# First expert slot narrowed to 64 places, the most loaded expert to 96, on raw weights

## The chip, the cores and the metric

The program runs on one core of a Trainium2 chip. The metric is the device time of one execution in microseconds (us), here the median of three runs. TensorE is called PE, VectorE DVE, ScalarE ACT, SyncE SP; SP issues all the DMA loads that matter here.

## The reference, cut to what matters

Two layers run over 256 latent tokens of width 1024. The change touches only the last part, the channel mixer of layer 1, a mixture of eight experts, each with three weight matrices of 1024 x 3584 float32:

```python
def moe_swiglu(x, w_router, w_gate, w_up, w_down):
    xt = x.reshape(-1, D)
    logits = (xt @ w_router).astype(jnp.float32)
    top_v, top_i = lax.top_k(logits, TOP_K)            # TOP_K = 2 of 8 experts
    top_w = jax.nn.softmax(top_v, axis=-1)
    gates = jnp.sum(jax.nn.one_hot(top_i, N_EXPERTS) * top_w[..., None], axis=1)
    y = jnp.zeros_like(xt)
    for e in range(N_EXPERTS):
        y = y + gates[:, e:e + 1] * swiglu(xt, w_gate[e], w_up[e], w_down[e])
    return y

def swiglu(x, w_gate, w_up, w_down):
    return (jax.nn.silu(x @ w_gate) * (x @ w_up)) @ w_down
```

All weights of all eight experts are read: 8 x 3 x 14.7 MB = 352 MB.

## The kernel before, in words

**Slots.** The experts are worked off in eight slots, one after the other. Slot 0 always holds expert 0, so that its weights can be loaded before the routing is known; slots 1 to 7 take the other experts by their token counts, the loads of these slots read the expert's number from a register on SP (`slot_expert`, a TENSOR_LOAD of `ordi`). The letters of `MODES` (L78) give each slot's width. L (wide) has 128 places; its weights are split by ACT and DVE (`split`, L168 and L169) into a high and a low float32r half, and PE multiplies three times (`mm3`, L232 to L234). S has 64 places, M has 96 (three groups of 32); both use the float32 weights as they were loaded ("raw"), with the tokens as the stationary side in 64 or 32 columns of the array and the weights streaming through it (`columns`, L1504). S and M are ranked: the smallest counts get S, the next M, the rest L. If a count is over the slot's places, a branch behind the slots (`tc.If(over > 0)`) runs all eight experts once more as wide ones for the rest of the tokens.

**Units.** A slot's weights come in 42 units of 1 MiB, 336 in all. Slot by slot and chunk by chunk (`CH`, columns of 1024, 1024, 1024, 512): gate, then up of a chunk (8 units, in the last chunk 4), then the down rows of the chunk before it (4 units, or 2). The last chunk's down units therefore stand behind the first gate and up of the next slot. PE goes through the units in that order; between them stand the transposes of the activations, the scatter of the previous slot's result, and the gather of the next slot's tokens, which are handed out one step per unit (`extras`).

**Buffers.** `moe_load` gives each unit a place in SBUF in the order that the generator `stages` yields. Places that lie there from the first eight units on are `wsx`, `hc`, `xgb0`, `xgb1`, `yh` and three called `wst2`, `wst4`, `wst5` (`ORDER`); the first unit lies in `sg` and `at`. Behind them `FILLS` names the places that come free when the attention layer ends. After that the loads go round the places: `RAW`, `yh` and `FIRSTS`, and, once the last wide slot's units are all loaded, also the three `wd` tiles, which until then hold the split halves. `yh` and `side1` leave the round after 40 units (`YHU`), because they are needed for results. A load can be issued only when the unit that lay in its place has been read to the end: by the split in a wide slot, by PE in a raw one. SP works off its loads in order.

**Order.** In this part of the program the order on each engine is the order in which the code is written (`manual_schedule` with `ROUTE` and `MOE`).

Of the kernel before, what the change touches and what calls it, by code (L numbers as in the profile page):

```python
# [8 lines left out]
def _quiet(msg, *args, **kwargs):  # L9
# [6 lines left out]
F32 = mybir.dt.float32  # L16
F32R = mybir.dt.float32r
I32 = mybir.dt.int32
AF = mybir.ActivationFunctionType
OP = mybir.AluOpType  # L20
# [3 lines left out]
P = 128  # L24
# [12 lines left out]
UNIT = 2048  # L37
# [15 lines left out]
LOOK = 2  # L53
NHALF = 5
HB = 5
FIRSTS = ('wst',) * 3 + ('xgb0', 'side0', 'wx', 'wst3', 'hx', 'side1', 'xgb1')
FILLS = 'wst wst hx0 wst xgb0 side0 wx wst3 hx1 side1'
LH = 5
RAW = ('wsx', 'wst5', 'hc', 'wst2', 'wst4')
ORDER = ('xgb0', 'xgb1', 'wsx', 'wst5', 'hc', 'wst2', 'wst4', 'yh')  # L60
PLACE = ('xgb', 'wst2', 'wst4', 'wst5', 'sg', 'at', 'yh')
TACT = 0, 2
# [8 lines left out]
BEGIN = "v a a n00 w0 s1 c t3 t2 m00 s1 a q3 a q2 W1 f n10 a n01 n11 b m10 a a n21 m01 s1 s1 a n20 n30 n31 a m11 a s1 m21 n41 a n40 m31 a w1 n51 m20 m30 s1 s1 n50 a m40 a n60 s1 s1 a n61 m41 m51 a m50 m60 m61 n70 n71 m71 m70"  # L71
START = {mybir.EngineType.PE, mybir.EngineType.SP}
WARM = 4, 4
YHU = 40
GY = 2
TMM = (3,)

MODES = "LSLMSMMS"  # L78
PARTS = {"S": (64, 1), "M": (32, 3)}
SLOTCAP = [P if m == "L" else PARTS[m][0] * PARTS[m][1] for m in MODES]  # L80
SLOTRANK = [-1] + [sum(MODES[1:].count(x) for x in "SML"[:"SML".index(m)]) + MODES[1:s + 1].count(m) - 1
                   for s, m in enumerate(MODES) if s]

# [48 lines left out]
def body(tc, nc, I, out, dbg=None):  # L132
    ctxs = []

    def pool(**kw):
        return tc.tile_pool(**kw)

    V, A, PE = nc.vector, nc.scalar, nc.tensor
# [3 lines left out]
    with top:  # L142
        con = top.enter_context(pool(name="con", bufs=1))
        psp = top.enter_context(pool(name="psum", bufs=1, space=PSUM))
        wst = top.enter_context(pool(name="wst", bufs=3))
        hpool = tc.tile_pool(name="hpool", bufs=1, side="right")
        hp = hpool.__enter__()
        cur = {}
# [88 lines left out]
        ph = top.enter_context(pool(name="all", bufs=1))  # L237
# [56 lines left out]
        hx = [ph.tile([P, 4, 256], F32, name=f"hx{i}", bufs=1) for i in range(2)]  # L294
        hc = ph.tile([P, DT, 256], F32, name="hc", bufs=1)
# [94 lines left out]
        G = [[con.tile([P, DT, 2], F32, name=f"G{l}{n}") for n in range(2)] for l in range(2)]  # L390
# [128 lines left out]
        def mod(l, i, d, s):  # L519
            return modT[l][:, 8 * i + d, s:s + 1]  # L520
# [131 lines left out]
        first = ada_first()  # L652
# [201 lines left out]
        for g in range(7):  # L854
# [15 lines left out]
            for which in ("g", "u"):  # L870
                if g == 0 and which == "g":
                    u = []
                    ps = []
# [17 lines left out]
                for fh in range(2):  # L891
                    u = stream.take(2)
                    feed(FEED.get((g, which, fh), 1))
                    for f2 in range(2):
                        ps = mm_ps()
# [221 lines left out]
        units = list(first_units)  # L1117
        early = {n: mp.tile([P, SIZES.get(n, UNIT)], F32, name=n, bufs=1) for n in PLACE}
# [13 lines left out]

        def stages():
            i = len(loaded)
            split_ends = max(j for j, u in enumerate(units) if u[0].mode == "L")
            for n in FIRSTS[FIRSTS.index("side1") + 1:]:
                i += 1
                yield n
            while True:
                for n in RAW + ("yh",) + FIRSTS + (("wd",) * (NHALF - 2) if i > split_ends else ()):  # L1140
                    if n == "wd" and "rest" in cur:
                        continue
                    if n != "wx" and (n not in ("yh", "side1") or i < YHU):
                        i += 1
                        yield n

# [62 lines left out]
        moe_stream = Halves(first_units)  # L1209
# [47 lines left out]
        side = ph.tile([P, 4096], F32, name="side", bufs=1)  # L1257
        early["side0"], early["side1"] = side[:, :UNIT], side[:, UNIT:]
        sums = early["side1"].rearrange("p (c d) -> p c d", c=2)
        early["wx"] = ph.tile([P, UNIT], F32, name="w", bufs=4)  # L1260
        early["hx"] = [ph.tile([P, UNIT // 2], F32, name=f"hx{i}", bufs=1) for i in range(2)]
        fills = FILLS.split()
        split_unit = source(units[len(loaded) + [n for n in fills if n != "hx0"].index("hx1")])
        parts = []
        for n in fills:
            if n[:2] == "hx":
                src, (k, n_) = split_unit
                i = int(n[2])
# [16 lines left out]
        for c in range(2):  # L1285
            V.scalar_tensor_tensor(lg[:, c, :], lgp[:, NE * c:NE * c + NE], rt[:, c:c + 1], wrb[:, 1, :],
                                   op0=OP.mult, op1=OP.add)
# [81 lines left out]

        def gather(ex, first=False):  # L1370
            if ex.mode != "L":
                yield from gather_raw(ex)
                return
            oh = s2t()[:, :2 * P].rearrange("p (c s) -> p c s", c=2)
            one_hot(oh, ex, 2)
            for _ in range(GY):
                yield
            xg = wtile().rearrange("p (i d s) -> p i d s", i=2, d=DT)
            ex.xg = xg
            n = 2 if first else 4  # L1380
            held = []
            for d0 in range(0, DT, n):
                tmp = s2t()[:, :n * P]
                ps = mm_ps() if first and d0 % 4 else tp_ps()
                for a in range(n):
                    for c in range(2):
                        h, d = divmod(d0 + a, 4)
                        PE.matmul(ps[:, a * P:(a + 1) * P], acct[c, h][:, d * P:(d + 1) * P], oh[:, c, :],
                                  start=(c == 0), stop=(c == 1))
                yield  # L1390
                for a in range(n):
                    dst, src, g, b = tmp[:, a * P:(a + 1) * P], ps[:, a * P:(a + 1) * P], G[1][1][:, d0 + a, 0:1], mod(1, 3, d0 + a, 0)
                    if first and a:
                        V.tensor_scalar(dst, src, g, b, op0=OP.mult, op1=OP.add)
                    else:
                        A.activation(dst, src, AF.Identity, bias=b, scale=g)
                tmp = tmp.rearrange("p (d s) -> p d s", s=P)
                A.copy(xg[:, 0, d0:d0 + n, :], tmp)
                held.append((d0, tmp))
                if not first or d0:  # L1400
                    low(xg, *held.pop(0))
                yield
            if first:
                low(xg, *held.pop(0))
                moe_stream.ahead(NHALF)
# [2 lines left out]
            n = tmp.shape[1]  # L1408
            V.tensor_sub(xg[:, 1, d0:d0 + n, :], tmp, xg[:, 0, d0:d0 + n, :])

        def gather_raw(ex):
            n = SLOTCAP[ex.col]
            oh = s2t()[:, :2 * n].rearrange("p (c s) -> p c s", c=2)
            one_hot(oh, ex, 2, n)
            for _ in range(GY):
                yield
            ex.tile = ph.tile([P, UNIT], F32, name="w", bufs=4)
            ex.xg = ex.tile[:, :DT * n].rearrange("p (d s) -> p d s", d=DT)
            for d0 in range(0, DT, 4):
                ps = tp_ps()  # L1420
                for d in range(d0, d0 + 4):
                    for c in range(2):
                        h, i = divmod(d, 4)
                        PE.matmul(ps[:, (d - d0) * n:(d - d0 + 1) * n], acct[c, h][:, i * P:(i + 1) * P], oh[:, c, :],  # L1424
                                  start=(c == 0), stop=(c == 1))
                yield
                scaled_rows(ex, ps, d0, 4, n)

        def back_raw(ex):
            dg = s2t().rearrange("p (a c t) -> p a c t", a=2, c=2)  # L1430
# [13 lines left out]
                V.scalar_tensor_tensor(ex.oht[:, i, :], held[:, :256], C("place" + ex.mode)[:, i:i + 1], held[:, 256:],  # L1444
                                       op0=OP.is_equal, op1=OP.mult)

        def scaled_rows(ex, ps, d0, k, n):
            for d in range(k):
                A.activation(ex.xg[:, d0 + d, :], ps[:, d * n:(d + 1) * n], AF.Identity,
                             bias=mod(1, 3, d0 + d, 0), scale=G[1][1][:, d0 + d, 0:1])  # L1450

        def gather_back(ex):
            if ex.mode != "L":
# [261 lines left out]
        with tc.manual_schedule(engines=MOE):  # L1715
# [4 lines left out]
            ex = order[-1]  # L1720
            y = scaled(ex)
            ps = {(c, h): tp_ps() if h else mm_ps() for c in range(2) for h in range(2)}
# [8 lines left out]
        with tc.If(over > 0):  # L1731
# [3 lines left out]
            rest = [Expert("L", e, [past, sel, selr, gates], e) for e in range(NE)]  # L1735
# [38 lines left out]
```

## Time and profile before

| | us |
|---|---|
| median of 3 runs | 1734.12 (1733.98 to 1734.18) |
| the profiled execution | 1732.13 |
| its span, first to last instruction | 1730.0 |
| granted PE clock over the span | 0.993 |
| PE busy | 1686.2 |
| DVE busy | 887.3 |
| ACT busy | 564.0 |
| read from HBM | 474.65 MB |

The busy time of PE is no measure of how full it is: a matmul that waits in the pipeline for its weights counts as busy. What tells the stages of the expert part apart is the rate of the DMA queues, and the times at which each slot gets through its first gate and up.

### The profile page before, as it was taken

The numbers are of one execution on the slowest core, as the hardware profiler recorded it, in microseconds if no ns is written. First come the engines' busy times: TensorE is split into PE (matmuls) and PEld (weight loads), VectorE is DVE, ScalarE is ACT, GpSimd is POOL, SyncE is SP. The second block draws the span as 40 slices with busy tenths as digits, with TensorE's granted clock in tenths as the row PEclk, the third lists the DMA queues.
The fourth block names the chain that finished last, engine by engine and source line by source line (L and its number), as shares of the span: only waits on it lengthen the run. The fifth ranks groups of instructions, "written<-read, shape, count | busy, mean of one in ns | idle before, by whom it ended". The sixth has DMA issues, their size and how long they took to land.

```text
span 1730.0 us, 32514 instructions
## 1 busy us (share of the span) xinstructions
PE 1686.2 (97%) x13735; PEld 1195.5 (69%) x13735; DVE 887.3 (51%) x1638; ACT 564.0 (33%) x1006; POOL 37.2 (2%) x33
## 2 busy tenths in 40 slices
PE   7999999999999999999899999999999999999997
PEld 4678988788787879979787447876654456656532
DVE  5579677767687767786887318862001010020021
ACT  4434532222222234685676126751000001001000
POOL 0000000000000000050000000000000000000000
PEclk9999999999999999999999999999999999999998
DMA  9765345544455432327888999999999999999994
GB/s 309 266 223 191 98 147 195 169 148 153 139 170 189 152 122 98 99 78 284 299 313 298 404 403 409 403 409 408 402 376 405 406 408 402 407 377 345 373 403 170
DMA packets 193736, 477.88 MB, mean 276 GB/s; under 512 B 9096, under 2 KB 68656, under 8 KB 192560
## 3 DMA queue, kind: packets, MB, share of 16 engines
q1 hardware_dynamic: 193584, 475.73, 74.8%
q8 instruction: 110, 1.80, 0.4%
q14 instruction: 42, 0.34, 0.1%
HBM read 474.65 MB, written 1.05 MB: 275 GB/s over the span
## 4 chain that ended last, share of the span: by engine, by line
PE 89%; DVE 4%; DMA 4%; issue 1%; ACT 1%; SPq 1%; POOL 0%; DVEq 0%; ACTq 0%
PE mm L1504 31%; PE mm L232 16%; PE mm L233 16%; PE mm L234 16%; PE tp L1424 1%; PE tp L1606 1%; DMA wst<-in_moe_w_gate_dram 1%; DMA xgb<-in_moe_w_gate_dram 1%; PE mm L1021 1%; PE mm L458 1%; PE tp L1555 1%; DVE wd L169 1%; DVE w L169 1%; DMA wst<-in_ada_w_dram 1%; DMA side<-in_ctx_dram 1%
## 5 line engine op out<-in xcount | busy, mean ns | idle before, releaser
L1688 DVE TENSOR_TENSOR sg<-sg,mm 128x512 f32<-128x512 f32 (+2 forms) x50 | 27.5, 580 | 408.3 <-PE mm L1504 408.3
L232 PE MATMUL mm<-b,w 128*128 128x512 f32 (+1 forms) x560 | 206.2, 368 | 0.0
L233 PE MATMUL mm<-b,w 128*128 128x512 f32 (+1 forms) x560 | 205.0, 366 | 0.0
L234 PE MATMUL mm<-b,w 128*128 128x512 f32 (+1 forms) x560 | 204.7, 366 | 0.0
L169 DVE TENSOR_TENSOR w<-wst,w 128x512 fp32r<-128x512 f32 (+1 forms) x201 | 145.2, 764 | 76.4 <-ACT w L168 76.0
L168 ACT CAST w<-wst 128x512 fp32r<-128x512 f32 (+1 forms) x201 | 127.5, 683 | 173.9 <-PE mm L233 129.8
L1504 PE MATMUL mm<-wst,w 128*32 128x256 f32 (+3 forms) x2544 | 177.1, 373 | 6.6 <-issue 6.6
L494 DVE SCALAR_TENSOR_TENSOR s<-wst,cT,s 128x512 f32<-128x512 f32 x224 | 153.3, 748 | 9.1 <-DMA wst<-in_ada_w_dram 9.1
L1504 PEld LDWEIGHTS mm<-wst,w 128*32 128x32 f32 (+1 forms) x2544 | 90.5, 115 | 79.2 <-issue 49.5
L1557 ACT COPY s<-tp 128x512 f32<-128x512 f32 (+2 forms) x33 | 16.4, 498 | 325.3 <-PE tp L1555 266.3
L232 PEld LDWEIGHTS mm<-b,w 128*128 128x128 f32 x560 | 105.7, 189 | 23.0 <-ACT side L168 4.2
L234 PEld LDWEIGHTS mm<-b,w 128*128 128x128 f32 x560 | 105.6, 189 | 17.0
L233 PEld LDWEIGHTS mm<-b,w 128*128 128x128 f32 x560 | 105.7, 189 | 16.7 <-DVE b L169 0.2
L1504 PE MATMUL mm<-wst,s 128*32 128x256 f32 (+1 forms) x1240 | 93.9, 403 | 1.3 <-issue 0.7
L232 PE MATMUL mm<-b,side 128*128 128x512 f32 (+1 forms) x240 | 90.9, 379 | 0.0
L234 PE MATMUL mm<-b,side 128*128 128x512 f32 (+1 forms) x240 | 90.2, 376 | 0.0
L233 PE MATMUL mm<-b,side 128*128 128x512 f32 (+1 forms) x240 | 90.0, 375 | 0.0
L232 PE MATMUL mm<-w,b 128*128 128x512 f32 (+1 forms) x224 | 79.3, 355 | 0.0
L233 PE MATMUL mm<-w,b 128*128 128x512 f32 (+1 forms) x224 | 78.1, 350 | 0.2 <-DVE w L169 0.2
L234 PE MATMUL mm<-w,b 128*128 128x512 f32 (+1 forms) x224 | 77.9, 348 | 0.0
L1504 PEld LDWEIGHTS mm<-wst,s 128*32 128x32 f32 (+1 forms) x1240 | 45.5, 113 | 45.6 <-issue 22.5
L1685 ACT ACTIVATE sg<-mm 128x512 f32<-128x512 f32 (+2 forms) x50 | 23.6, 510 | 149.8 <-PE mm L1504 149.8
(402 smaller groups left out, 3059.0 us busy)
## 6 DMA issues: line engine op xcount, KB each, us to landing
wst<-in_moe_w_gate_dram SPq DMA_DIRECT2D x55, 1024.0 KB, 13.2
wst<-in_moe_w_up_dram SPq DMA_DIRECT2D x51, 1024.0 KB, 14.1
wst<-in_moe_w_down_dram SPq DMA_DIRECT2D x51, 1024.0 KB, 14.8
wst<-in_ada_w_dram SPq DMA_DIRECT2D x40, 1024.0 KB, 5.2
xgb<-in_moe_w_gate_dram SPq DMA_DIRECT2D x18, 1024.0 KB, 11.7
wst<-in_ffn_w_gate_dram SPq DMA_DIRECT2D x14, 1024.0 KB, 5.0
wst<-in_ffn_w_up_dram SPq DMA_DIRECT2D x14, 1024.0 KB, 5.0
wst<-in_ffn_w_down_dram SPq DMA_DIRECT2D x14, 1024.0 KB, 5.1
```

The lines of the kernel that those rows point to most:

```text
L168: A.copy(hi, src)
L169: V.tensor_sub(lo, src, hi)
L232: PE.matmul(ps, sh, mh, start=start, stop=False)
L233: PE.matmul(ps, sh, ml, start=False, stop=False)
L234: cur["pe"] = PE.matmul(ps, sl, mh, start=False, stop=stop).ins
L458: PE.matmul(ps[j:j + 32, :], ones[:, :32], acc_[s], start=True, stop=True)
L494: V.scalar_tensor_tensor(acc_[s], u[:, k, :], c_, acc_[s], op0=OP.mult, op1=OP.add)
L1021: PE.matmul(ps[64 * par:64 * par + 64, :256], vt[:, kc, 64 * kvh:64 * kvh + 64], pT[:, kc, par].rearrange("p a b -> p (a b)"), start=(kc = ...
L1424: PE.matmul(ps[:, (d - d0) * n:(d - d0 + 1) * n], acct[c, h][:, i * P:(i + 1) * P], oh[:, c, :], start=(c == 0), stop=(c == 1))
L1504: PE.matmul(ps[n * g:n * g + n, c0:c0 + w], x, wrow[:, w * g:w * g + w], start=start and first, stop=stop and last)
L1685: A.activation(x, p, AF.Silu)
L1688: V.tensor_mul(x, x, p)
```

## The change

`MODES` goes from `LSLMSMMS` to `SMSMMSMS`: slot 0 gets 64 places instead of 128, slot 1 96 instead of 64, slot 2 64 instead of 128. No wide slot is left in the normal course, so no expert weight is split. The `wd` tiles hold raw units from the start, and a second `w` tile (`wy`) takes one unit of the first filling. The round of places becomes one table (`CYCLE`), and `LEAVE` says after how many units a place leaves it: `yh` after 70, `side1` after 40. The first gather goes through `gather_raw`; its eight evictions with scale and bias alternate between DVE and ACT.

```diff
-FIRSTS = ('wst',) * 3 + ('xgb0', 'side0', 'wx', 'wst3', 'hx', 'side1', 'xgb1')
-FILLS = 'wst wst hx0 wst xgb0 side0 wx wst3 hx1 side1'
+CYCLE = ('xgb0', 'xgb1', 'wsx', 'wst5', 'hc', 'wst2', 'wst4', 'yh', 'wst', 'wst', 'wst', 'wd', 'wd', 'wd', 'side0', 'wst3',
+         'hx', 'side1')
+FILLS = 'wst wst hx0 wst wd wd wd side0 wx wy wst3 hx1 side1'
-RAW = ('wsx', 'wst5', 'hc', 'wst2', 'wst4')
-YHU = 40
+LEAVE = {'yh': 70, 'side1': 40}
-MODES = "LSLMSMMS"
+MODES = "SMSMMSMS"
...
-                for n in RAW + ("yh",) + FIRSTS + (("wd",) * (NHALF - 2) if i > split_ends else ()):
-                    if n == "wd" and "rest" in cur:
+                for n in CYCLE:
+                    if n == "wd" and (i <= split_ends or "rest" in cur):
                         continue
-                    if n != "wx" and (n not in ("yh", "side1") or i < YHU):
+                    if i < LEAVE.get(n, i + 1):
                         i += 1
                         yield n
...
-        early["wx"] = ph.tile([P, UNIT], F32, name="w", bufs=4)
+        for n in ("wx", "wy"):
+            early[n] = ph.tile([P, UNIT], F32, name="w", bufs=4)
...
-        def scaled_rows(ex, ps, d0, k, n):
+        def scaled_rows(ex, ps, d0, k, n, first):
             for d in range(k):
-                A.activation(ex.xg[:, d0 + d, :], ps[:, d * n:(d + 1) * n], AF.Identity,
-                             bias=mod(1, 3, d0 + d, 0), scale=G[1][1][:, d0 + d, 0:1])
+                dst, src, g, b = ex.xg[:, d0 + d, :], ps[:, d * n:(d + 1) * n], G[1][1][:, d0 + d, 0:1], mod(1, 3, d0 + d, 0)
+                if first and d % 2 == 0:
+                    V.tensor_scalar(dst, src, g, b, op0=OP.mult, op1=OP.add)
+                else:
+                    A.activation(dst, src, AF.Identity, bias=b, scale=g)
```

SP's queue at the end of the attention layer, where the places of the first filling come free (`hx` is half a unit, the numbers only tell tiles apart). Before:

```order
L179 DMA hx_7210<-in_moe_w_down_dram 128x1024
L179 DMA wst<-in_moe_w_gate_dram 128x2x1024
L179 DMA xgb<-in_moe_w_up_dram 128x2x1024
L179 DMA side<-in_moe_w_up_dram 128x2x1024
L179 DMA w<-in_moe_w_up_dram 128x2x1024
L179 DMA wst_7222<-in_moe_w_up_dram 128x2x1024
L179 DMA hx_7211<-in_moe_w_down_dram 128x1024
L179 DMA side<-in_moe_w_down_dram 128x2x1024
L179 DMA xgb<-in_moe_w_down_dram 128x2x1024
L179 DMA wsx<-in_moe_w_down_dram 128x2x1024
```

The same place now:

```order
L179 DMA hx_7196<-in_moe_w_down_dram 128x1024
L179 DMA wst<-in_moe_w_gate_dram 128x2x1024
L179 DMA wd<-in_moe_w_up_dram 128x2x1024 x3
L179 DMA side<-in_moe_w_up_dram 128x2x1024
L179 DMA w<-in_moe_w_down_dram 128x2x1024 x2
L179 DMA wst_7214<-in_moe_w_down_dram 128x2x1024
L179 DMA hx_7197<-in_moe_w_down_dram 128x1024
L179 DMA side<-in_moe_w_gate_dram 128x2x1024
L179 DMA xgb<-in_moe_w_gate_dram 128x2x1024 x2
L179 DMA wsx<-in_moe_w_gate_dram 128x2x1024
```

Three `wd` loads and one more `w` load have come in ahead of the first reuse of `xgb`, and that reuse, which was second in this queue behind a split, now stands behind PE's reading.

ACT's queue from the routing (`routed`) to the first activation of slot 0 (`sg`). Before, with the casts of the split (L168) in between:

```order
L1317 ACTIVATE routed<-lg,rs 128x8 x2
L1396 ACTIVATE s_7267<-tp,modT_157,G_161 128x128
L1398 CAST w<-s_7267 128x256
L1396 ACTIVATE s_7276<-mm,modT_157,G_161 128x128
L1398 CAST w<-s_7276 128x256
L1396 ACTIVATE s_7286<-tp,modT_157,G_161 128x128
L1398 CAST w<-s_7286 128x256
L1396 ACTIVATE s_7296<-mm,modT_157,G_161 128x128
L168 CAST wd<-xgb 128x1024
L1398 CAST w<-s_7296 128x256
L168 CAST wd<-wsx 128x1024 x2
L168 CAST w<-wst_6834 128x1024 x2
```

The same place now:

```order
L1315 ACTIVATE routed<-lg,rs 128x8 x2
L1453 ACTIVATE w<-tp,modT_157,G_161 128x64 x4
L1688 ACT_TABLE_LOAD
L1688 ACTIVATE sg<-mm 128x512
L1560 COPY s_7369<-tp 128x512
```

Four evictions of the gather are left between the routing and the first activation; every cast of weights is gone, and on DVE the subtractions that went with them.

## Rows read from the trace of the kernel before

**Rows 1.** The page: the span, and GB/s in 40 equal slices of it.
```profile
span 1730.0 us, 32514 instructions
...
GB/s 309 266 223 191 98 147 195 169 148 153 139 170 189 152 122 98 99 78 284 299 313 298 404 403 409 403 409 408 402 376 405 406 408 402 407 377 345 373 403 170
```

**Rows 2.** Stretches: length, busy us and counts by engine, clock, DMA share, GB/s.
```profile
804.30:850.00 45.70, 41.82 (x247) 35.89 (x246) 35.14 (x76) 29.38 (x43) 0.72 (x1) 1.00 0.84 299
850.00:961.20 111.20, 110.41 (x515) 84.83 (x516) 84.07 (x84) 73.42 (x85) 0.00 (x0) 0.98 0.85 305
...
1178.90:1297.80 118.90, 115.30 (x1891) 69.66 (x1887) 11.57 (x25) 10.34 (x25) 0.00 (x0) 1.00 1.01 394
...
1517.70:1638.90 121.20, 118.81 (x1979) 69.64 (x1971) 10.63 (x25) 9.30 (x23) 0.00 (x0) 1.00 0.97 362
```

**Rows 3.** Timeline of DVE, the products after up: start, length, instruction, [idle before].
```profile
850.05 1.28 DVE L1688 TENSOR_TENSOR sg<-sg,mm 128x512 f32<-128x512 f32 x2
...
961.18 0.69 DVE L1688 TENSOR_TENSOR sg<-sg,mm 128x512 f32<-128x512 f32 x1 [0.67 <-PE mm L1504]
...
1059.44 1.28 DVE L1688 TENSOR_TENSOR sg<-sg,mm 128x512 f32<-128x512 f32 x2
...
1178.89 1.02 DVE L1688 TENSOR_TENSOR sg<-sg,mm 128x512 f32<-128x512 f32 x2 [3.89 <-PE mm L1504]
1208.97 1.02 DVE L1688 TENSOR_TENSOR sg<-sg,mm 128x512 f32<-128x512 f32 x2 [8.56 <-PE mm L1504]
...
1297.83 0.69 DVE L1688 TENSOR_TENSOR sg<-sg,mm 128x512 f32<-128x512 f32 x1 [24.30 <-PE mm L1504]
1323.47 0.69 DVE L1688 TENSOR_TENSOR sg<-sg,mm 128x512 f32<-128x512 f32 x1 [5.03 <-PE mm L1504]
1350.23 0.69 DVE L1688 TENSOR_TENSOR sg<-sg,mm 128x512 f32<-128x512 f32 x1 [24.14 <-PE mm L1504]
1364.74 0.42 DVE L1688 TENSOR_TENSOR sg<-sg,mm 128x256 f32<-128x256 f32 x1 [13.82 <-PE mm L1504]
1392.42 1.02 DVE L1688 TENSOR_TENSOR sg<-sg,mm 128x512 f32<-128x512 f32 x2 [27.26 <-PE mm L1504]
1420.35 1.02 DVE L1688 TENSOR_TENSOR sg<-sg,mm 128x512 f32<-128x512 f32 x2 [8.10 <-PE mm L1504]
...
1517.67 1.02 DVE L1688 TENSOR_TENSOR sg<-sg,mm 128x512 f32<-128x512 f32 x2 [30.87 <-PE mm L1504]
...
1638.88 0.69 DVE L1688 TENSOR_TENSOR sg<-sg,mm 128x512 f32<-128x512 f32 x1 [25.48 <-PE mm L1504]
```

**Rows 4.** The chain that ended last: start, us, what; DMA from issue to landing.
```profile
820.38 0.91 PE tp L1388 x8
...
860.47 0.23 PE mm L232
...
893.23 1.73 PE tp L1424 x16
...
1014.17 17.37 DMA xgb<-in_moe_w_gate_dram
...
1316.34 7.02 PE mm L1504 x32
...
1410.14 10.50 PE mm L1504 x192
...
1715.29 0.69 DVE s L1596
```

**Rows 5.** Timeline of SP, two loads: start, length, instruction.
```profile
804.29 0.37 SPq L179 DMA_DIRECT2D wst<-in_moe_w_gate_dram  x1
...
813.91 0.37 SPq L179 DMA_DIRECT2D side<-in_moe_w_up_dram  x1
```

**Rows 6.** DMA issues: count, KB each, median us from issue to landing.
```profile
wst<-in_b_w_out_dram SPq DMA_DIRECT2D x4, 1024.0 KB, 5.2
```

**Rows 7.** Groups by form after 880 us: count, busy us, mean ns, idle before.
```profile
L169 DVE TENSOR_TENSOR wd<-wst,wd 128x1024 fp32r<-128x1024 f32 x44 | 53.4, 1222 | 14.0 <-ACT wd L168 13.2
```

More of the change, by code (lines that the diff above doesn't have):

```diff
@@ L1134, in stages @@
             i = len(loaded)
[L1135 to L1138, printed above, removed]
+            split_ends = max((j for j, u in enumerate(units) if u[0].mode == "L"), default=0)
             while True:
-                for n in RAW + ("yh",) + FIRSTS + (("wd",) * (NHALF - 2) if i > split_ends else ()):
-                    if n == "wd" and "rest" in cur:
+                for n in CYCLE:
+                    if n == "wd" and (i <= split_ends or "rest" in cur):
                         continue
-                    if n != "wx" and (n not in ("yh", "side1") or i < YHU):
+                    if i < LEAVE.get(n, i + 1):
                         i += 1
@@ L1371, in gather @@
             if ex.mode != "L":
-                yield from gather_raw(ex)
+                yield from gather_raw(ex, first)
                 return
@@ L1409, in low, with gather_raw @@
             V.tensor_sub(xg[:, 1, d0:d0 + n, :], tmp, xg[:, 0, d0:d0 + n, :])
-        def gather_raw(ex):
+        def gather_raw(ex, first):
             n = SLOTCAP[ex.col]
@@ L1426, in gather_raw @@
                 yield
-                scaled_rows(ex, ps, d0, 4, n)
+                scaled_rows(ex, ps, d0, 4, n, first)
+            if first:
+                moe_stream.ahead(NHALF)
         def back_raw(ex):
```

## The prediction

> **What bounds the kernel now.** I read the rate of the loads first, because 352 MB of expert weights must pass. In the page's slices [rows 1] the rate lies at 402 to 409 GB/s from about 950 us to 1510 us, but for one slice at 376; stretch by stretch it is 299 GB/s before the first product and 305 GB/s through slot 0 [rows 2]. So in the first expert the loads aren't the limit; something else gives the places free too slowly. Then I read the moments at which each slot's first gate and up are done, which are the starts of the first product on DVE in each slot: 850.0, 961.2, 1059.4, 1178.9, 1297.8, 1392.4, 1517.7 and 1638.9 us [rows 3]. From one to the next are 111.1 (slot 0, wide), 98.3 (S), 119.5 (wide), 118.9 (M), 94.6 (S), 125.3 (M), 121.2 (M) and 91.1 us to the end of the span at 1730.0.
>
> What sets these lengths comes from the pitches in the chain [rows 4]. A wide unit is 12 matmuls of 0.23 us, 2.76 us. A raw S unit is a quarter of 7.02 us, 1.755 us; a raw M unit a quarter of 10.50 us, 2.625 us. A unit's load, 1.0486 MB at the mean of the full slices, 405.5 GB/s, takes 2.586 us. So wide and M slots are paced by PE, S slots run faster than the loads and win back what the others lost. Slot 0 holds the loads back: 42 units at 2.76 us, with only the few places that a split has emptied. Behind it slot 1 (S) eats up the stock, and PE stands: the chain has a load of 17.4 us at 1014.2 us [rows 4]. From there on PE is always a little behind the loads, and at the end the loads wait for places again (362 GB/s in slot 6 [rows 2]). The time after 1060 us is therefore PE's sum, and the time before it is lost in slot 0.
>
> **The change part by part.**
>
> Splits: two wide slots had 84 units, two halves each; 168 subtractions of 1.22 us [rows 7] go from DVE, and as many casts from ACT. They stand on the path only while the first chunk waits for them, up to 850 us; later PE hides them. They are worth nothing of their own beyond the start of slot 0.
>
> Start of slot 0: the gather's matmuls begin at 820.4 us [rows 4], as before, because nothing ahead of them changes on the path. Two groups of 16 rows at 1.73 us (the nearest row is the 64-place gather at 893.2 us [rows 4]) end at 823.9 us. The eight evictions alternate between DVE and ACT and depend on each other. No row shows one of 64 columns; it can't be dearer than a product of 512 columns, 0.7 us [rows 3], and each sets free a row of weights for which PE needs 0.88 us (half a unit). So the bounds are 0, if PE's pace hides all but the first, which falls under the second gather group, and 8 x 0.7 = 5.5 us, if none hides; I take 0. Eight S units (the first chunk's gate and up, landed long before) take 14.0 us, the step to DVE 0.7 us [rows 3]: first product at 838.5 us instead of 850.0, a gain of 11.5 us.
>
> Slot 0 as S: slot 4, an S slot before an M slot, shows the stretches: 25.6, 26.8, 14.5 and 27.7 us [rows 3]. Its first holds two down units and the scatter of an M slot, which slot 0 has not behind anything; eight units and a transposition cost what its third stretch costs, 14.5 us. Slot 0 takes 14.5 + 26.8 + 14.5 + 27.7 = 83.5 us, 27.6 less than 111.1.
>
> Slot 1 as M between two S slots: slot 3 (M, next is S) took 118.9 us, of which the first stretch, with a wide slot's rest in it, 30.1 us; behind an S slot (slot 5) that stretch took 27.9 us [rows 3]. So 116.8 us, 18.5 more than slot 1 took. Slot 2 as S between two M slots is slot 4's case: 94.6 us, 24.9 less than 119.5.
>
> Slots 3 to 7: the letters are now M M S M S where they were M S M M S, so the same spans stand in another order: 125.3, 121.2, 94.6, and for slot 6 116.8 instead of 118.9; the last 91.1 us stay. That is 2.1 us less.
>
> Loads: after the `wst` load at 804.3 us [rows 5] nothing held three `wd` loads back, and with them the queue has four units, 10.3 us of work, until `side` comes free at 813.9 us [rows 5]. So I take the loads as running without a gap from 804.3 us. By then 12.5 units are issued; the thirteenth lands at 809.5 us by the 5.2 us that a load into an empty queue takes [rows 6], and unit n at 809.5 + 2.586 x (n - 12.5). The first reuse of a place (`xgb0`, the second unit) waits for PE at 827.5 us, and the 21 units filled before it keep the queue busy until 831.5 us. The register load for slot 1 stands in SP's queue behind the 40th unit, which waits for PE's 22nd, some 26 us after the first product; DVE writes the numbers within slot 0's first units, one gating step per unit, so no load queued behind it is late. If that cover were gone, the loads would stop, and PE has over 10 us of stock there.
>
> Is the stock enough? PE needs unit 132 at 1133.4 us by the sum below, and it lands at 1118.5 us; unit 258 is needed at 1474.5 and would land at 1444.4; the last at 1666 and 1646. Where PE falls over 40 us behind (around slot 4, unit 216: 1379.9 against 1335.7 us) the loads wait for places, some 10 us, which costs the stock and not PE. PE is starved only when the mean pitch of the loads is over 2.65 us, (1666 - 809.5) / 323.5.
>
> [...]
>
> The sum: 838.5 + 83.5 + 116.8 + 94.6 + 125.3 + 121.2 + 94.6 + 116.8 + 91.1 = 1682.4 us of span, 47.6 less than 1730.0. The profiled execution took 2.1 us more than its span (1732.1), so 1684.5; the median of the runs shown, 1734.1, lies 2.0 above that, so **1686.5 us**.
>
> **The rivals.**
>
> Loads become the pace. With all slots raw, PE has little left over the loads, 20 us at the end without holds. Slot 3 shows a slower pitch in a busy stretch, 394 GB/s or 2.66 us [rows 2]. If that held throughout, the last unit lands at 809.5 + 323.5 x 2.66 = 1670 us, and one unit and the tail (1730.0 - 1715.3 [rows 4]) make 1686.6, so 1690.7 us on the median's scale; at 2.70 us it is 1703.6. Against it: the slices with a full queue, 402 to 409 GB/s [rows 1], are 2.56 to 2.61 us.
>
> The loads' pace falls far, and the kernel is slower. Raw slots put all loads, PE's short matmuls and their instructions side by side from 825 us on, and the rate in slot 6 was 362 GB/s, 2.90 us a unit [rows 2]. If this is what a raw M slot does to the loads, and not the lack of places, the end is 809.5 + 323.5 x 2.90 + 16.5 = 1764, or 1768 us. It decides from 2.79 us a unit (375 GB/s) on, where the sum reaches 1730. Against it: slot 5, also M, lies in slices of 402 to 408 GB/s [rows 1]. [...]
>
> The stock is richer than thought and PE a little quicker. The M spans that I borrowed may hold losses that don't recur; if the four M slots take 2 us less each (their spans here differ by up to 6) and one of the two gather groups is hidden, the end is near 1673, or 1677 us. The loads alone would allow 1667.
>
> The change doesn't do what it says. The branch behind the slots runs eight wide experts when a count is over its places. The reference's router on its own inputs gives the eight experts 64, 77, 60, 41, 36, 75, 88 and 71 tokens: expert 0 just fits its 64, the four largest of the others fit 96, the rest 64. The closest choice between second and third expert is 0.003 in the logits. One token more on expert 0 and the run costs eight times 111 to 120 us more, some 2600 us.
>
> **How the numbers follow.** Forecast 0.70, loads as a mild pace 0.15, quicker 0.10, loads far slower 0.03, branch 0.02. What a measurement of this kernel can tell from no change is about 0.2%, 3.5 us. The first three are all faster, 0.95; the other two slower, 0.05; of the first I give 0.01 to no change. The range goes from the quick end, 1677 us, to the loads at 2.70 us, 1704 us.
>
> **What would show it.** Right: first product at about 838 us; slot spans of 83, 117, 95, 125, 121, 95 and 117 us; over 400 GB/s from 805 us to about 1330 us, with a dip around slot 4 only; no L168 or L169 on expert weights, and ACT and DVE mostly idle after 825 us. The mild rival shows as waits of PE for loads in slots 2, 5 or 7, and the slower one as a rate under 375 GB/s with SP not waiting for PE. A branch that ran would show L232 to L234 behind slot 7. The forecast is wrong by its own terms if S or M spans differ here from the ones I borrowed, above all slot 0's and slot 1's, which I have not seen in that place.

## The result, and the profile after

The changed kernel takes 1689.62 us (median of four runs, 1688.92 to 1690.11) where the kernel before takes 1734.15 us: a ratio of 0.9743, with a 95% interval from 0.9726 to 0.9760. The forecast was 1686.5 us, the range 1677 to 1704 us. Five more runs of it on another chip gave 1689.67 us.

Its page answers [rows 1]. First the span, the busy time of PE and the rate of the loads in 40 equal slices, and the queue that will matter later:

```profile
span 1687.4 us, 35070 instructions
...
PE 1643.7 (97%) x15290; PEld 1099.5 (65%) x15290; DVE 677.7 (40%) x1451; ACT 386.6 (23%) x823; POOL 37.2 (2%) x33
...
GB/s 310 280 222 183 120 126 199 150 160 158 131 175 174 178 147 100 86 78 213 379 404 408 406 403 390 403 408 408 402 407 371 343 372 403 409 407 402 408 405 204
...
q8 instruction: 122, 2.00, 0.5%
```

The span fell from 1730.0 to 1687.4 us, 42.6 us. The slices at 284 to 313 GB/s of [rows 1] are gone. From 844 us on the rate is over 400 GB/s but for three slices from 1266 to 1392 us, the dip at slot 4 that was foreseen, one at 390 and the last.

The starts of the first product in each slot, on DVE's timeline, answer [rows 3]; two later products of slot 1 stand among them:

```profile
838.34 0.69 DVE L1691 TENSOR_TENSOR sg<-sg,mm 128x512 f32<-128x512 f32 x1 [7.63 <-PE mm L1507]
854.95 0.69 DVE L1691 TENSOR_TENSOR sg<-sg,mm 128x512 f32<-128x512 f32 x1 [9.43 <-PE mm L1507]
...
922.69 1.02 DVE L1691 TENSOR_TENSOR sg<-sg,mm 128x512 f32<-128x512 f32 x2 [27.26 <-PE mm L1507]
...
988.25 1.02 DVE L1691 TENSOR_TENSOR sg<-sg,mm 128x512 f32<-128x512 f32 x2 [33.84 <-PE mm L1507]
1015.98 0.71 DVE L1691 TENSOR_TENSOR sg<-sg,mm 128x256 f32<-128x256 f32 x2 [26.71 <-PE mm L1507]
1041.33 0.69 DVE L1691 TENSOR_TENSOR sg<-sg,mm 128x512 f32<-128x512 f32 x1 [24.64 <-PE mm L1507]
1135.92 1.02 DVE L1691 TENSOR_TENSOR sg<-sg,mm 128x512 f32<-128x512 f32 x2 [27.26 <-PE mm L1507]
1261.19 1.02 DVE L1691 TENSOR_TENSOR sg<-sg,mm 128x512 f32<-128x512 f32 x2 [32.54 <-PE mm L1507]
1382.38 0.69 DVE L1691 TENSOR_TENSOR sg<-sg,mm 128x512 f32<-128x512 f32 x1 [25.92 <-PE mm L1507]
1476.97 1.02 DVE L1691 TENSOR_TENSOR sg<-sg,mm 128x512 f32<-128x512 f32 x2 [27.26 <-PE mm L1507]
1596.28 0.69 DVE L1691 TENSOR_TENSOR sg<-sg,mm 128x512 f32<-128x512 f32 x1 [24.91 <-PE mm L1507]
```

The differences are the slots' lengths:

| | first product | slot 0 | 1 | 2 | 3 | 4 | 5 | 6 | tail | span |
|---|---|---|---|---|---|---|---|---|---|---|
| before | 850.05 | 111.1 | 98.3 | 119.5 | 118.9 | 94.6 | 125.3 | 121.2 | 91.1 | 1730.0 |
| predicted | 838.5 | 83.5 | 116.8 | 94.6 | 125.3 | 121.2 | 94.6 | 116.8 | 91.1 | 1682.4 |
| after | 838.34 | 84.3 | 118.6 | 94.6 | 125.3 | 121.2 | 94.6 | 119.3 | 91.1 | 1687.4 |

So of the 42.6 us, 11.7 came before the first product and 26.8 in slot 0. Slots 1 and 2 together (217.7 before, 213.2 after) gave 4.5 us, the four slots behind them lost 0.4.

Stretch by stretch, in the columns of [rows 2], the loads run without the gap that slot 0 used to make:

```profile
804.30:838.00 33.70, 33.62 (x212) 22.29 (x212) 13.09 (x53) 9.16 (x20) 0.72 (x1) 1.00 1.01 389
838.00:922.00 84.00, 83.15 (x710) 37.69 (x712) 4.24 (x11) 7.84 (x18) 0.00 (x0) 1.00 1.03 406
922.00:1038.00 116.00, 112.40 (x1877) 66.41 (x1871) 10.23 (x23) 9.30 (x23) 0.00 (x0) 0.99 1.02 399
...
1258.00:1380.00 122.00, 119.41 (x2027) 70.86 (x2017) 10.65 (x24) 9.41 (x23) 0.00 (x0) 1.00 0.97 360
```

389 GB/s where [rows 2] had 299, 406 where it had 305; DVE is busy for 4.2 us of slot 0 where it was for 84. But look at PE in slot 1: 112.4 of 116 us busy, 3.6 us idle, though it is the engine that paces this slot. The chain names no releaser for them ("issue"); it also shows the gather ahead of the first product, which answers [rows 4]:

```profile
820.14 3.52 PE tp L1422 x32
823.66 1.87 PE mm L1507 x8
...
1002.62 3.18 PE mm L1507 x108
1005.80 1.10 issue
1006.90 3.70 PE mm L1507 x128
1010.60 2.49 issue
1013.10 13.75 PE mm L1507 x242
```

These pauses stand among the 128-column matmuls of an M slot's last, 512-wide chunk. They stand where slots 1 and 6 run over the forecast, and the later experiments are on them.

### The profile page after: what moved, and what is told of

Its sections match the earlier page's. It is cut to its first block, busy times and chain, and to the rows that moved or that the text cites. A ratio compares the mean times of both kernels' runs of the same rounds, so it can differ in the third digit from the quotient of the medians.

```text
span 1687.4 us, 35070 instructions
## 1 busy us (share of the span) xinstructions
PE 1643.7 (97%) x15290; PEld 1099.5 (65%) x15290; DVE 677.7 (40%) x1451; ACT 386.6 (23%) x823; POOL 37.2 (2%) x33
## 4 chain that ended last, share of the span: by engine, by line
PE 93%; DVE 2%; DMA 2%; issue 1%; ACT 1%; POOL 0%; SPq 0%; DVEq 0%; ACTq 0%
PE mm L1507 44%; PE mm L232 13%; PE mm L233 13%; PE mm L234 12%; PE tp L1422 2%; PE tp L1609 2%; PE tp L1558 1%; DMA wst<-in_ada_w_dram 1%; PE mm L1021 1%; PE mm L458 1%; DMA side<-in_ctx_dram 1%; PE tp L1006 1%; PE tp L1437 1%; PE mm L430 0%; DMA side<-in_x_dram 0%
## 5 line engine op out<-in xcount | busy, mean ns | idle before, releaser
L1507 PE MATMUL mm<-wst,w 128*32 128x256 f32 (+2 forms) x3120 | 219.3, 380 | 7.4 <-issue 7.4
L1507 PEld LDWEIGHTS mm<-wst,w 128*32 128x32 f32 (+1 forms) x3120 | 111.2, 115 | 101.4 <-issue 56.0
L168 ACT CAST w<-wst 128x512 fp32r<-128x512 f32 x172 | 97.3, 620 | 169.5 <-PE mm L233 129.6
L169 DVE TENSOR_TENSOR w<-wst,w 128x512 fp32r<-128x512 f32 x172 | 110.3, 686 | 63.0 <-ACT w L168 62.5
L1560 ACT COPY s<-tp 128x512 f32<-128x512 f32 (+2 forms) x44 | 21.9, 498 | 460.5 <-PE tp L1558 381.8
L233 PEld LDWEIGHTS mm<-b,w 128*128 128x128 f32 x560 | 105.7, 189 | 16.6 <-DVE b L169 0.2
L1507 PE MATMUL mm<-wst,s 128*32 128x256 f32 (+1 forms) x1432 | 114.1, 408 | 2.0 <-issue 1.5
L1507 PE MATMUL mm<-wd,w 128*32 128x256 f32 (+2 forms) x1160 | 93.3, 402 | 0.0
L1507 PEld LDWEIGHTS mm<-wst,s 128*32 128x32 f32 (+1 forms) x1432 | 55.1, 114 | 54.4 <-issue 27.7
## 6 DMA issues: line engine op xcount, KB each, us to landing
wst<-in_moe_w_gate_dram SPq DMA_DIRECT2D x44, 1024.0 KB, 15.1
```

The costliest lines, as they stand in the source:

```text
L168: A.copy(hi, src)
L169: V.tensor_sub(lo, src, hi)
L233: PE.matmul(ps, sh, ml, start=False, stop=False)
L1507: PE.matmul(ps[n * g:n * g + n, c0:c0 + w], x, wrow[:, w * g:w * g + w], start=start and first, stop=stop and last)
L1560: A.copy(dst, pt[:, :len(bs) * P])
```

## Experiments

Twelve kernels, each timed beside the kernel before on its chip. The theory: nearly all of the gain is slot 0's width, with the splits at its start; from there on PE paces the slots. "The M slots" are slots 1, 3, 4 and 6.

**Slot 0 wide, the most loaded expert raw** (one half of the change undone).

```diff
-FILLS = 'wst wst hx0 wst wd wd wd side0 wx wy wst3 hx1 side1'
+FILLS = 'wst wst hx0 wst side0 wx wst3 hx1 side1'
-LEAVE = {'yh': 70, 'side1': 40}
+LEAVE = {'yh': 40, 'side1': 40}
-MODES = "SMSMMSMS"
+MODES = "LMSMMSMS"
...
-        for n in ("wx", "wy"):
+        for n in ("wx",):
```

> Slot 0 wide again (modes L M S M M S M S), the other slots as changed; the first filling without wd and wy, and yh leaves the round after 40 units, as a wide slot needs it. My theory (PE's work sets the end behind slot 0, slot 0's narrowing is nearly the whole gain): first product near 850 us, slot 0 about 118 us (111.1 of before plus 8 units of M instead of S at 0.87 us), then M 121, S 95, 125, 121, 95, 119 and 91: a span near 1733 us, so no gain left against before. Rival (the loads set the end once no other wide slot is there): loads run full from about 955 us with unit 54, the last lands near 955 + 282 x 2.586 = 1684, a span near 1701 us.

Measured: 1739.17 us, ratio 1.0029 [1.0019, 1.0039], span 1736.0, 3 us over the theory's 1733 and far from the rival's 1701. Its products:

```profile
849.41 1.28 DVE L1691 TENSOR_TENSOR sg<-sg,mm 128x512 f32<-128x512 f32 x2
...
967.11 1.02 DVE L1691 TENSOR_TENSOR sg<-sg,mm 128x512 f32<-128x512 f32 x2 [3.89 <-PE mm L1507]
...
1087.80 0.69 DVE L1691 TENSOR_TENSOR sg<-sg,mm 128x512 f32<-128x512 f32 x1 [25.75 <-PE mm L1507]
```

The first product is where [rows 3] has it, slot 0 takes 117.7 us. Making the most loaded expert raw gives nothing without the narrow slot 0; it even costs 0.3%.

**Slot 0 narrow, the most loaded expert wide** (the other half undone: `MODES = "SLSMMSMS"`).

> Only slot 1, with the most loaded expert, wide and split (modes S L S M M S M S); all else as changed. My theory: a wide slot costs PE less than an M slot, 112 to 113 us from an S to an S slot (2 x 1.755 + 32 x 2.76 + 8 x 1.755 and some 7 us between the units, as before's slot 2 had) against 118.6 measured, and leaves some 3 us less to the slot behind it; slot 0 gets 1 us longer: a span near 1680 us, 7 to 8 us less than the changed kernel. Rival 1 (the splits and the three places that they take hold the loads back, so raw weights pay for the most loaded expert too): 1690 to 1700 us. Rival 2 (the loads set the end): 1687 us, the same.

Measured: 1688.00 us, ratio 0.9731 [0.9718, 0.9744], span 1685.0: the whole gain. Slot 1 takes 115.7 us, 3.0 less than raw, and PE makes no pause in it. The loads ran at 386 GB/s beside it, and a later row of the chain leads to one of them:

```profile
1110.15 4.85 PE mm L1507 x85
1115.00 19.00 DMA wd<-in_moe_w_down_dram
...
1134.04 1.94 PE mm L1507 x8
```

A row like this one says that a load was the last thing waited for, not that PE stood for its 19 us: all of PE's waits for loads in slots 1 to 4 come to 0.8 us. So the theory was right on where the gain lies and too hopeful by 5 us (1680 expected), but hardly for the stock that the first rival named. Some 3 us of the 5 are slot 1 itself, which was put at 112 to 113 us; slots 3 and 4 took 2.8 us more than in the changed kernel, and PE's waits put down to issue in slot 4 were 2.0 us longer (4.4 against 2.4). With the run before it, the change has a working half, the first slot's width; the other half, which makes the last wide slot raw, is worth nothing that these runs can tell.

**Slot 0 narrow, the wide slot third** (`MODES = "SSLMSMMS"`).

> Slot 0 narrow and raw as in the changed kernel, but the most loaded expert stays wide, now as slot 2, with its split halves. So only the half of the change that makes the first slot narrow. Theory (slot 0 carries the gain, and a wide slot among raw ones costs PE what an M slot costs): first product at 838 us, slot 2 about 120 us, span 1682 to 1690 us. Rival (the raw most loaded slot is a good part of the gain): 1700 us or more.

Measured: 1697.88 us, ratio 0.9789 [0.9776, 0.9802], span 1696.1. The theory's 1682 to 1690 failed, and the rival's 1700 or more was not reached either, for a reason that neither named. Slot 2, the wide one, took 119.4 us as the theory had it; slot 1 took 107.4 us. Two S slots in a row outran the loads: from 916 to 1024 us PE is idle for 10.6 of 108 us while the loads run at 407 GB/s, and the chain is on them:

```profile
956.03 18.18 DMA side<-in_moe_w_gate_dram
...
977.86 17.89 DMA wst<-in_moe_w_gate_dram
...
1003.56 17.80 DMA wsx<-in_moe_w_gate_dram
```

Not the widths alone count but their order. The predicted kernel sets an M slot behind slot 0, in which the loads, at 2.586 us a unit, gain on PE's 2.625.

**The first filling cut short** (`wd` three times, `wy` left out of it).

```diff
-FILLS = 'wst wst hx0 wst wd wd wd side0 wx wy wst3 hx1 side1'
+FILLS = 'wst wst hx0 wst side0 wx wst3 hx1 side1'
-        for n in ("wx", "wy"):
+        for n in ("wx",):
```

> As changed, but the first filling leaves out the three wd loads and the second w load, so that the load queue runs dry from about 808 to 814 us and 17 instead of 21 units lie ready. My theory (PE has 13 to 20 us of stock wherever it is tightest, so a later load costs nothing): a span of 1687 to 1689 us. Rival (the loads set the end): the 6 to 9 us that the queue stands empty come out at the end, 1694 to 1696 us.

Measured: 1692.46 us, ratio 0.9754 [0.9741, 0.9767], span 1688.6. The loads had run at 269 instead of 389 GB/s up to the first product, and yet every slot but slots 3 and 4 took what it took above to 0.2 us (slot 0 84.3, slot 1 118.6, slot 2 94.6 us). The span is the theory's, not the rival's 1694 to 1696. The profiled execution lost 1.2 us, the median 2.8, with ratios whose intervals overlap. The stock ahead of slot 0 hardly matters; PE's pace does.

**Evictions on one engine** (all eight of the first gather on ACT).

```diff
-                if first and d % 2 == 0:
+                if False:
```

> The changed kernel with all eight evictions of the first gather on ACT instead of every other one on DVE. Theory (evictions lie beside PE's work): ACT needs 8 x 0.40 = 3.2 us where PE needs 0.88 us per row, so the first product stays within 0.5 us of 838.3 us and the span within 1 us of 1687 us. Rival (the chain of evictions sets the first product): 2 us or more later.

Measured: 1688.46 us, ratio 0.9738 [0.9723, 0.9752], span 1686.0. ACT's timeline and DVE's first product:

```profile
821.96 1.29 ACT L1453 ACTIVATE w<-tp,modT,G 128x64 f32<-128x64 f32 x4 [1.99 <-PE tp L1422]
823.74 1.29 ACT L1453 ACTIVATE w<-tp,modT,G 128x64 f32<-128x64 f32 x4 [0.50 <-PE tp L1422]
...
838.39 0.69 DVE L1691 TENSOR_TENSOR sg<-sg,mm 128x512 f32<-128x512 f32 x1 [7.64 <-PE mm L1507]
```

Four evictions take 1.29 us on one engine. In the changed kernel, where they alternate and each waits for the one before it, they were no quicker:

```profile
823.70 0.34 DVE L1451 TENSOR_SCALAR w<-tp,G,modT 128x64 f32<-128x64 f32 x1 [0.62 <-PE tp L1422]
824.08 0.40 ACT L1453 ACTIVATE w<-tp,modT,G 128x64 f32<-128x64 f32 x1 [0.57 <-DVE w L1451]
824.52 0.34 DVE L1451 TENSOR_SCALAR w<-tp,G,modT 128x64 f32<-128x64 f32 x1 [0.47 <-ACT w L1453]
824.90 0.40 ACT L1453 ACTIVATE w<-tp,modT,G 128x64 f32<-128x64 f32 x1 [0.41 <-DVE w L1451]
```

From the second gather's end, 823.66 us, PE multiplies without a wait while the last four evictions are still to come. Their cost is zero either way.

**Half of each load** from slot 3 on.

```diff
+HALVED = 3
...
+                if u[0].col >= HALVED:
+                    src, shape = src[:, :shape[0] // 2], (shape[0] // 2, shape[1])
...
+                    return [v, v]
```

> As changed, but from slot 3 on only half of each unit is loaded (and used twice), so the result is not the reference's; PE's instructions are the same. My theory (PE sets the end): slots 3 to 7 keep their spans, 125, 121, 95, 119 and 91 us, and the total stays within 2 us of 1687 us, but for what the short pauses of PE in the last chunk of each M slot (1 to 2.6 us each, some 4 us a slot, put down to issue) owe to the busy load queues: if they come from instructions fetched beside full loads, up to 12 us go. Rival (the loads set the end): the end falls until PE's own work shows, 15 us or more, with the S slots shrinking as well.

Measured: 1676.73 us, ratio 0.9664 [0.9646, 0.9682], span 1675.2. Slot 5 (S), in which PE goes through the units fastest, stays at 94.59 us to the digit, so it had not waited for loads. Most of what fell is the third stretch of slots 3, 4 and 6, from 26.5, 24.1 and 28.2 to 22.5, 22.4 and 22.8 us; slot 1, whose loads were whole, kept its 27.7. PE's waits put down to issue come to 0.2 us from slot 3 to slot 6, with a DMA share of 0.60 to 0.62 in slots 3, 4 and 6 where it was 0.97 to 1.03: the pauses went with the full load queues. Two causes fit: PE's instructions come late beside full queues, or PE reads SBUF more slowly beside the loads' writes.

**The short matmuls in two bursts.**

```diff
...
+            if up_last(ex, w):
+                down(*pend, at)
             ps = gate_up(ex, w)
...
-                down(*pend, at)
+                if not up_last(ex, w):
+                    down(*pend, at)
```

> The changed kernel, but in the last, 512-wide chunk of each M slot the four `up` units of 128-column matmuls stand behind the two `down` units of the chunk before, not ahead of them, so that the short matmuls come in two bursts instead of one of four units. Theory (PE's pauses come from its instructions being brought in beside full load queues, and a short burst outruns less of its stock): the third or fourth stretches of slots 1, 3, 4 and 6 lose some of their 1.1 and 2.5 us pauses, 5 to 10 us in all, span 1678 to 1682 us. Rival (the pauses go with the number of short matmuls, in whatever order): stretches shift but slot spans stay at 118.6, 125.3, 121.2 and 119.3 us, span 1687 us.

Measured: 1686.85 us, ratio 0.9726 [0.9712, 0.9739], span 1683.9. The M slots took 115.1, 124.6, 121.8 and 118.9 us, 4.0 less in all, most of it in slot 1. This is between theory and rival: a burst half as long helps a little at most (the changed kernel's M slots differ by 1.3 us in all between its two profiles), and most of the pauses stay.

**The same, and transposes later.**

```diff
...
-                for _ in range(-(-len(steps) // units_left)):
+                for _ in range(-(-len(steps) // units_left) if k0 >= late * per else 0):
...
```

> The last kernel, and in slot 0 the transposes of chunk 1 begin one unit later, so that PE does not wait for them right behind the first product. Theory: slot 0's first stretch goes from 16.6 us to about 14.9 us and the span falls by about 1.7 us against the last kernel, unless loads are late behind it; rival (the wait is only moved to a later step): slot 0 stays at 84 us.

Measured: 1685.49 us, ratio 0.9724 [0.9711, 0.9738], span 1683.0. Slot 0's first stretch:

```profile
838.82 0.69 DVE L1698 TENSOR_TENSOR sg<-sg,mm 128x512 f32<-128x512 f32 x1 [7.64 <-PE mm L1512]
854.51 0.69 DVE L1698 TENSOR_TENSOR sg<-sg,mm 128x512 f32<-128x512 f32 x1 [9.43 <-PE mm L1512]
```

15.69 us instead of 16.61, a gain of 0.92 where 1.7 was expected. The 1.7 us were read from the row of the weight loads, idle there for 1.73 us where the matmuls are for 0.85; PE itself stood only from 838.2 to 839.1 us.

**Up and down units mixed one by one** (gate, gate, down, up, down, up, down, down in an M slot's last chunk; else as the kernel before).

```diff
...
+                next(between, 0)
                 u = unit()
...
+            between = down_steps(*pend, at) if up_last(ex, w) else iter(())
+            next(between, 0)
+            ps = gate_up(ex, w, between=between)
+            for _ in between:
+                pass
...
```

> The kernel with the late transposes and the moved up units, but up units and the down units of the chunk before are mixed one by one: gate, gate, down, up, down, up, down, down. Theory (the rate of instruction packets is the limit): this stretch has 384 rows of 128 and 192 of 256 columns, 576 rows or 4.5 packets in 21.5 us, where 6 us each make 27 us; the mix alone takes no rows away, so the M slots gain nothing more than 1 us each over the kernel before, span 1680 to 1684 us. Rival (only long bursts outrun the stock): the pauses go, M slots 113 to 119 us, span 1675 to 1678 us.

Measured: 1685.53 us, ratio 0.9726 [0.9712, 0.9739], span 1683.1. The four M slots took 118.0, 124.5, 120.0 and 118.0 us, 480.5 in all as in the run with two bursts and late transposes (480.4). A finer mix gives nothing, as the theory had it: with the same instructions in the stretch, their order matters little.

**Half as many matmuls, twice as wide.**

```diff
...
+                    b = min(w * g, wrow.shape[-1] - m * w)
+                    PE.matmul(ps[n * g:n * g + n, c0:c0 + m * w], x, wrow[:, b:b + m * w],
...
+                    if raw and ex.mode == "M" and w == CH[-1]:
+                        if k % 2 == 0:
...
```

> The changed kernel, but the gate and up units of each M slot's last, 512-wide chunk issue half as many matmuls of 256 columns instead of 128: every second row of the weights is left out and each other row's slice is read twice as wide, so PE's columns and all loads stay as they are (half of these products is left out, half is computed for nothing). Theory (a 16 KB packet of PE's instructions holds 128 rows and comes in only every 6 us beside full load queues, while 128 rows of 128 columns last 3.7 us): the pauses of 1.1 and 2.5 us go with the loads as full as before, third stretches of slots 1, 3, 4 and 6 fall from 24 to 28 us to 22 to 23 us, span 1674 to 1678 us. Rival (the pauses come from PE reading SBUF beside the loads' writes): nothing falls, span 1687 us.

Measured: 1675.20 us, ratio 0.9665 [0.9647, 0.9682], span 1673.5. The chain at the place of the pauses, and two products:

```profile
1003.43 18.27 PE mm L1508 x336
```

```profile
989.10 1.02 DVE L1696 TENSOR_TENSOR sg<-sg,mm 128x512 f32<-128x512 f32 x2 [33.85 <-PE mm L1508]
1011.04 0.72 DVE L1696 TENSOR_TENSOR sg<-sg,mm 128x256 f32<-128x256 f32 x2 [20.93 <-PE mm L1508]
```

No pause: from the first product to slot 7 PE's waits put down to issue are gone, where the changed kernel has 15.1 us of them. The third stretches of all four M slots take 21.95 us, with as many columns through PE and full loads. So it is the number of instructions, and not how many columns PE reads. Not all that fell is pauses: with half loads, where there were next to none, the third stretches of 128-column matmuls still took 22.4 to 22.8 us. How instructions come in, the instruction queue shows. First the changed kernel over the 740 us from 860 us on: the stretch's row, with PE's matmuls and weight loads in the second and third place, and the queue's row (packets, MB, share of the DMA engines' time):

```profile
860.00:1600.00 740.00, 724.79 (x10278) 397.07 (x10278) 60.35 (x132) 59.57 (x144) 0.00 (x0) 1.00 1.02 397
```

```profile
q8 instruction: 81, 1.33, 0.7%
```

And the same two rows of this kernel:

```profile
860.00:1600.00 740.00, 740.00 (x9630) 383.11 (x9626) 65.86 (x143) 61.20 (x146) 0.00 (x0) 1.00 1.03 404
```

```profile
q8 instruction: 76, 1.25, 0.7%
```

10278 matmuls and as many weight loads are 20556 instructions in 81 packets of 16.4 KB (1.33 MB in all), 254 to a packet; for the other, 19256 in 76 packets, 253. From pause to pause the chain of the changed kernel has 126 to 128 matmuls, with their weight loads 252 to 256 instructions, so one packet's worth; 128 matmuls of 128 columns take 3.70 us. In the changed kernel three packets begin between 1004 and 1017 us, at 1004.3, 1010.6 and 1016.8 us, 6.3 and 6.2 us apart, with q1, the loads, at 95% of the DMA engines' time; with half loads, at 49%, four begin in the 13 us from 1215.5 us on, so at most 4.3 us apart in the mean. In the changed kernel each of the nine pauses of 1.0 us and more ends 2.4 to 2.6 us after a packet has begun: the two in the chain further up end at 1006.90 and 1013.10 us, behind the packets of 1004.3 and 1010.6. The two queues in these stretches, first the changed kernel, then the one with half loads:

```profile
q1 hardware_dynamic: 1294, 4.93, 95.0%
q8 instruction: 3, 0.05, 1.5%
```

```profile
q1 hardware_dynamic: 579, 2.10, 48.9%
q8 instruction: 4, 0.07, 2.0%
```

One packet took 1.04 us in either case (1.5% of 16 engines' 13 us for three, 2.0% for four). What fills the rest of the 6.3 us, and when a packet is asked for, no row here shows.

What the instructions gave was not all kept. The M slots fell by 22.2 us in all, the span by 13.9. At the end of this kernel PE waits for the loads:

```profile
1616.68 19.35 DMA wst<-in_moe_w_gate_dram
...
1638.10 18.57 DMA wst<-in_moe_w_down_dram
```

Here the loads become the pace, as the prediction's first rival had it, but only after PE had come 21 us ahead of the changed kernel (slot 7's first product at 1574.9 against 1596.3 us); the last stretch gives 7.4 us of that back.

**Two bursts, late transposes, and the wide slot 1** (`MODES = "SLSMMSMS"` on top).

> The late transposes and moved up units together with the most loaded expert on split weights in slot 1 (only slot 0 narrow). Theory (the raw most loaded slot brings nothing of its own): within 3 us of the kernel that has the most loaded expert raw, span 1680 to 1686 us. Rival (a raw most loaded slot is better once the pauses are fewer): 1687 us or more.

Measured: 1682.05 us (1681.57 to 1682.70, five runs), ratio 0.9705 [0.9692, 0.9719], span 1679.4. In the same batch the changed kernel had this:

> The changed kernel as it is, on the same chip as the three others, so that differences of 1 to 5 us can be told: span 1686 to 1689 us by every theory.

Measured: 1689.67 us (1688.38 to 1690.41, five runs), ratio 0.9748 [0.9734, 0.9761], span 1686.2. So this version beats both kernels, the changed one by 7.6 us. Against the kernel with two bursts, late transposes and a raw slot 1 (span 1683.0, on another chip) it gains 3.6 us of span, a little more than the theory's 3. Slot 1 itself is no shorter than there (115.7 against 115.1 us), but PE makes no pause in it (busy for all of the 116 us from 922 us on): a wide unit has fewer instructions, 12 matmuls against 48 of an M unit of a full chunk and 96 of its last chunk's. PE's waits put down to issue come to 5.4 us in all where they were 11.7; why they are shorter in the later slots too, no run shows.

## Why the prediction was right, point by point

**The start.** First product at 838.34 us against 838.5 (the terms as they stand add up to 838.6). The gather took 3.52 us against 3.46, the evictions nothing, which was the end of the bounds that was taken.

**Slot 0** 84.3 us against 83.5. The first stretch was mis-sized, 16.6 against 14.5: 0.9 us is PE's wait for the transposes that stand right behind the first product, and 1.1 us the back gather's matmuls, which stand here and make the second stretch 1.2 us shorter than the borrowed one. The term at fault is the one that borrows "what its third stretch costs" for a stretch that has other steps in it.

**Slots 1 and 6** 118.6 and 119.3 us against 116.8. The first two stretches are the borrowed ones to 0.1 us (27.93 and 37.63). Most of the difference is in the third, 27.7 and 28.2 where the borrowed slot had 26.3, the rest in the fourth. It is not the pauses alone: they come to 3.6 us in slot 1 as in the borrowed slot, and to 4.2 in slot 6. Behind the second pause of slot 1 the matmuls up to the end of the unit took 2.3 us, in the borrowed slot 1.2; no row shows why. The third stretches differ from run to run too (26.4 and 26.5 us in the run on the other chip). The borrowed M spans held such pauses already, and the rival "quicker" was right that they held losses, but here they recurred. Slots 2 to 5 and the tail came to 0.1 us as borrowed.

**The sum** was short by 5.0 us of span: 0.9 of slot 0, 1.8 and 2.5 of slots 1 and 6, less 0.2 at the start. The median was missed by 3.1 only, because the step from the profiled execution to the median, taken as 2.0 us, was 0.1 here. That is luck: it depends on which execution was profiled.

**Slot 0 and PE's waiting.** One reading of the kernel before was wrong. The prediction has slot 1 eat up a stock that slot 0 left small, "and PE stands", from a load of 17.4 us in the chain. The row of that slot 1, in the columns of [rows 2], has PE busy for 97.0 of 98.2 us:

```profile
961.20:1059.40 98.20, 96.99 (x480) 50.09 (x480) 30.93 (x38) 28.23 (x40) 0.00 (x0) 1.00 1.03 407
```

Its 1.2 us of waits are for split halves that come after that load. In slot 0 PE was busy for 110.4 of 111.2 us [rows 2]. So that slot 0 holds the loads back cost PE next to nothing; what the change takes away behind the first product is PE's own work on the units of slot 0, 1.755 us each where a wide one takes 2.76. The sum was added up from slot lengths and did not use this reading, so it stood.

**Loads without a gap** held: 389 GB/s up to the first product and 399 to 406 in slots 0 to 3, with 360 in slot 4 alone. The run with the short filling shows that this part could have been worse by a third ahead of the first product and cost little. **The mild rival** did not occur in the changed kernel; it appears where PE runs 21 us ahead of that, and where two S slots stand in a row.

**What the splits cost** was put at nothing beyond the start of slot 0. The run with a wide slot 1 bears it out: PE was busy for all of the 116 us from 923 us on, so the splits cost it no wait there. At the start of slot 0, in the kernel before, PE's last matmul ends at 846.2 us and DVE is at its subtractions until the product begins at 850.05, so they cost 3.8 us there. The runs change a slot's width and its splits together and don't part the two further. What the prediction did not see is that a wide slot is 3 us quicker than a raw M slot with its pauses (115.7 against 118.6 us). Without the pauses the raw one would be ahead: with half as many matmuls in the last chunk slot 1 took 112.65 us.

## What to carry to other kernels

When one engine paces a chain of stages, price the change in the stage that changes and borrow the others' lengths from slots with the same neighbours; that came within 5 of 43 us here. Before you read a load in the chain as an engine's wait, look at that engine's idle time: 17.4 us of load stood beside 1.2 us of waiting. Where an engine that paces a stage is idle with no releaser, count its instructions beside the packets of the instruction queue: here many short matmuls beside full load queues were bound by their number, and half as many of twice the width, not a finer order, took 15.1 us of pauses away. And look at what is next in line before valuing a gain: 22 us taken off PE gave 14, since the loads ended last then.

## What the runs showed of the hardware that was not expected

PE's instructions come in over a DMA queue, q8: in the changed kernel from 860 to 1600 us 20556 matmuls and weight loads in 81 packets of 16.4 KB, 254 to a packet. They came more slowly beside full loads: three packets began in the 13 us from 1004 us on, with the loads at 95% of the DMA engines' time, and four in 13 us at half loads, at 49%. Around the pauses of slot 1 the packets began 6.0 to 6.3 us apart (998.3, 1004.3, 1010.6 and 1016.8 us), where 128 matmuls of 128 columns with their weight loads last 3.70 us. Not every gap was so long: in slot 4, with the loads at 94%, two packets began 3.7 us apart (1347.3 and 1351.0 us). Four units of such matmuls made each M slot 3.5 to 6.7 us longer than half as many of 256 columns did. With those in their place (7.0 us for 128) no pause was left; in the changed kernel two of the nine, of 1.23 and 1.25 us, stand among the 256-column down matmuls right behind the short ones.
